# Moving eight background steps of a two-mixer encoder layer to later stages

## The chip, the core and the metric

The kernel runs on one core of a Trainium2 chip. Each engine of a core has a queue of its own and works it off in order: TensorE (PE) multiplies and transposes, VectorE (DVE), ScalarE (ACT) and GpSimd (POOL) do elementwise work, SyncE (SP) issues the DMA transfers. Where an instruction needs what another engine makes, it waits for a semaphore, and everything behind it on its own queue waits too. The metric is the time of one execution in microseconds (us), the median of several runs.

## The reference, cut to what matters

One layer is computed for a prompt of 1024 rows and a sample of 32 rows, width 1024, all in float32:

```
u  = RMSNorm(h) @ w_in                      # 1024 x 4096: q k v g for A and for B
oA = softmax(band(qA kA^T / 8 + bias)) vA   # 8 heads of 64, own chunk of 64 and 8 chunks back
oB = stick_breaking(qB kB^T / 8) vB         # 8 heads of 64, strictly causal:
     # w = sigmoid(z) * product of sigmoid(-z) over the later keys
y  = [oA * silu(gA), oB * silu(gB)] @ w_out
h  = h + RMSNorm(y)
h  = h + sigmoid(h @ w_ple_gate) * (p @ w_ple)
```

The new keys and values are outputs too. The sample rows attend to a cache of 512 keys.

## The kernel before

Float32 products are made of float32r products: each operand is split into a high and a low part, and three of the four products of parts are added (`mms`, L732; `multiply`, L1566).

The work has three parts. First the rows are normalised and turned, and the first three projections made. Then come eight *stages*, one for each head set in `pairs` (L1197): A0, B0, A1, B1, A2, B2, A3, B3. A head set is two heads of one mixer; two neighbouring stages (an A and a B) are a pair of head sets. Stage n holds the attention of head set n for both heads, and beside it the projections (`mm_...`) of head set n+1; stage 7 has the eight gate blocks (`mm_gA`, `mm_gB`) beside it. In the stages with an odd second number (2, 3, 6, 7) the attention of the sample rows is put in as well (`with_sample`, L1336). The third part makes the two large products with `w_out` and `w_ple_gate`.

For each row block of 128 queries the attention makes scores (`SA`, `SB`, L825), weights (`om`, `be`), the turned weights (`weights_t`, L871) and the product with the values (`PVA`, `PVB`). Most weight blocks are turned by PE: transposes into a bank `ptwA` or `ptwB`, then ACT casts the high part (`wTh`) and DVE subtracts the low part (`wTl`). There are two such banks. Row block 5 of A and blocks 4 and 6 of B (`ROUND`, L31) are turned through DRAM instead: DVE turns 32 x 32 squares, SP stores the result (`swapA<-om`) and loads it back with four transfers (`be<-swapA`), then ACT casts it.

The third part computes each product from quarters of the weights with seven instead of eight products of blocks (`ORDER`, L1499). For this it needs four sums and differences of the weight's quarters, T1 to T4. They are made beforehand, beside the attention, by eight steps: `sum_weights(w, kt)` (L1303) for `w` = "o" (`w_out`) and "g" (`w_ple_gate`) and `kt` = 0 to 3. A step loads four quarter slices of 128 x 512 (tiles `oB...` or `gB...`, buffers of the tag `sg`, of which there are three), does four subtractions or additions on POOL, each in two pieces of 128 x 256, and stores the four results to `sum_dr` in DRAM. The pieces have a lower standing than other POOL work (`rec.low = 1`). The buffers of the tag `sg` are later those of the gates' products (L754) and of the slices that the third part loads.

Two lists are merged for each stage (`weave`, L1265): `att`, the attention's steps, and `den`, the projections' steps, in proportion to the work that each entry states. The steps of weight sums are entries of `att` with stated work 0, at places 8 and 28 (`with_sums`, L1328).

Nothing is issued at once. All operations are recorded (`Recorder`, L265) and put in order by a planner (`order`, L381): it goes through all engines in planned time with stated costs, takes on each engine the ready operation of the best standing, and counts DVE and POOL work that shares a port one after the other. SP's transfers are planned as one line. The engines then execute in the planned order. So a step that is moved changes the order of nearly everything behind it. All instructions go through one line of the emitting function, L461, so the profile names groups by tile and not by line.

Of the kernel before, what the change touches and what calls it, by code (L numbers as in the profile page):

```python
# [466 lines left out]
def stream_step(  # L467
# [797 lines left out]
    def weave(att, den):  # L1265

        ta = sum(x[0] for x in att) or 1.0
        td = sum(x[0] for x in den) or 1.0
        ia = idn = 0
        pa = pd = 0.0  # L1270
        while ia < len(att) or idn < len(den):
            take_a = ia < len(att) and (idn >= len(den) or RATE * pa / ta <= pd / td)
            if take_a and att[ia][2] and any(x in prep for x in att[ia][2]):
                assert idn < len(den)
                take_a = False
            if not take_a and len(den[idn]) > 2 and den[idn][2]:
                take_a = ia < len(att)
            if take_a:
                rec.cls = 0
                att[ia][1]()  # L1280
                pa += att[ia][0]
                ia += 1
            else:
                rec.cls = 1
                den[idn][1]()
                pd += den[idn][0]
                idn += 1
            rec.cls = 0
            prepare()


    SUMS = {"T1": 0, "T2": 1, "T3": 2, "T4": 3}
    QUARTERS = {"B11": (0, HALF[0]), "B12": (0, HALF[1]), "B21": (4, HALF[0]), "B22": (4, HALF[1])}

    def weight_part(w, key, kt):
        if key in SUMS:
            return sum_dr[w][kt, SUMS[key]]
        k0, cols = QUARTERS[key]
        if w == "g":
            return w_gate[0].rearrange("(p k) c -> k p c", k=KD)[k0 + kt][:, cols]  # L1300
        return w_out[0, (k0 + kt) * P:(k0 + kt + 1) * P, cols]

    def sum_weights(w, kt):  # L1303
        b = {}

        def sub(out, x, y, op):
            rec.low = 1
            for c in (slice(0, 256), slice(256, 512)):
                nc.gpsimd.tensor_tensor(out[:, c], x[:, c], y[:, c], op)
            rec.low = 0  # L1310

        for key in ("B12", "B22", "B11", "B21"):
            b[key] = at2.tile([P, 512], F32, tag="sg", name=f"{w}{key}{kt}", bufs=3)
            rec.hold(b[key])
            dma(b[key], weight_part(w, key, kt))
            if key == "B22":
                sub(b[key], b[key], b["B12"], ALU.subtract)
                dma(sum_dr[w][kt, 2], b[key])
            if key == "B11":
                sub(b["B12"], b["B12"], b[key], ALU.subtract)  # L1320
                dma(sum_dr[w][kt, 0], b["B12"])
                sub(b[key], b["B22"], b[key], ALU.add)
                dma(sum_dr[w][kt, 1], b[key])
            if key == "B21":
                sub(b[key], b["B11"], b[key], ALU.subtract)
                dma(sum_dr[w][kt, 3], b[key])

    def with_sums(att, todo):  # L1328
        out = list(att)
        for i, (w, kt) in enumerate(todo):  # L1330
            out.insert(8 + i * 20, (0.0, lambda w=w, kt=kt: sum_weights(w, kt), None))
        return out
# [3 lines left out]
    def with_sample(att, steps):  # L1336
        out = list(att)
        for at_, st in reversed(list(zip(SAMPLE_AT, steps))):
            out.insert(at_, (st[0], st[1], None))
        return out  # L1340
# [67 lines left out]
    for n in range(8):  # L1408
        den = []
        for j in range(*span[n + 1]):  # L1410
            den += col_steps(j)
        att = seq[n, 0] + seq[n, 1]
        if pairs[n][1] % 2 == 1:
            att = with_sample(att, sample_attention(pairs[n][0], pairs[n][1] // 2))
        if n < 4:
            att = with_sums(att, [("og"[n // 2], 2 * (n % 2) + i) for i in range(2)])
        weave(att, den)


# [446 lines left out]
```

## Time and profile before

| | |
|---|---|
| median of 3 runs | 788.48 us (788.15 to 789.07) |
| the profiled execution | 791.73 us |
| its span | 789.9 us |
| PE / DVE / ACT / POOL busy | 777.9 / 590.3 / 532.2 / 472.3 us |
| granted clock of TensorE | 0.999 |
| data moved by DMA | 153.66 MB, mean 195 GB/s |

The profiled execution has its own time, a little above the median, and its span runs from the first instruction to the last. The page gives busy times by engine, the span in 40 slices with the busy share of each engine in tenths, the DMA queues, the chain of work that ended last, and the costliest groups of instructions. In a group, the figures behind the first bar are the busy time and the mean of one instruction in ns, and those behind the second are the engine's idle time just before them and what ended it. Idle time on an engine counts only if PE, busy for nearly the whole span, comes to wait for it.

### The profile page before, as it was taken

To read this page: it belongs to the slowest core of one execution; us is meant where nothing else is said; L and a number is where in the kernel's file an instruction comes from. 1 tells how busy PE (TensorE), PEld (TensorE's weight loads), DVE (VectorE), ACT (ScalarE), POOL (GpSimd) and SP (SyncE) were. 2 spreads that over 40 slices of the span, in tenths; PEclk is the share of its full clock that TensorE was granted. 3 is DMA by queue.
4 is the path that set the end of the run, shared out by engine and by line. 5 is a ranking of instruction groups with operands and counts; after the bars stand their busy time and mean duration, and the time that the engine had idled before them with its cause. 6 is when DMAs were issued, how large, how long until landed. Compare 5 with 4: busy or idle time off the path is not lost.

```text
span 789.9 us, 14445 instructions
## 1 busy us (share of the span) xinstructions
PE 777.9 (98%) x4606; PEld 718.7 (91%) x4606; DVE 590.3 (75%) x1105; ACT 532.2 (67%) x1169; POOL 472.3 (60%) x554
## 2 busy tenths in 40 slices
PE   9999999999999999999999999999999999999997
PEld 7999989999999999999999999999998787888786
DVE  7717677897788887777979778884464677988965
ACT  6636786786687766887677787753336966777651
POOL 5615776865677677644645465565562529599523
PEclk9999999999999999999999999999999999999999
DMA  8419876757786858743525756655588865859754
GB/s 303 133 41 276 207 219 188 223 150 221 201 238 207 226 174 250 162 122 119 146 65 173 175 133 183 186 165 164 144 275 287 277 190 186 298 164 345 273 161 134
DMA packets 161086, 153.66 MB, mean 195 GB/s; under 512 B 38561, under 2 KB 127177, under 8 KB 161010
## 3 DMA queue, kind: packets, MB, share of 16 engines
q1 hardware_dynamic: 161010, 152.73, 65.3%
q8 instruction: 37, 0.61, 0.3%
q14 instruction: 39, 0.32, 0.1%
HBM read 94.45 MB, written 49.83 MB: 183 GB/s over the span
## 4 chain that ended last, share of the span: by engine, by line
PE 86%; DVE 3%; ACT 3%; DMA 3%; POOL 2%; issue 1%; SPq 1%; ACTq 0%; DVEq 0%
PE mm_gB L461 6%; PE mm_gA L461 6%; PE mm_kB L461 5%; PE mm_qA L461 5%; PE mm_kA L461 5%; PE mm_vA L461 5%; PE mm_qB L461 5%; PE PVB L461 4%; PE mm_vB L461 4%; PE SA L461 4%; PE SB L461 4%; PE PVA L461 3%; PE ptwB L461 3%; PE g1P L461 2%; PE o3P L461 2%; PE o1P L461 2%
## 5 line engine op out<-in xcount | busy, mean ns | idle before, releaser
L461 POOL TENSOR_TENSOR be<-be,om 128x256 f32<-128x256 f32 (+8 forms) x66 | 81.6, 1240 | 66.2 <-DVE om L461 51.9
L461 DVE TENSOR_TENSOR_SCAN om<-om,SB 128x384 f32<-128x384 f32 (+5 forms) x96 | 92.2, 965 | 16.2 <-ACT be L461 7.6
L461 POOL TENSOR_SCALAR be<-be,statA 128x640 f32<-128x640 f32 (+3 forms) x64 | 45.0, 708 | 28.6 <-DVE statA L461 21.0
L461 ACT ACTIVATE om<-SB 128x384 f32<-128x384 f32 (+5 forms) x96 | 47.3, 499 | 20.7 <-DVE SB L461 15.7
L461 ACT ACTIVATE be<-SB 128x384 f32<-128x384 f32 (+5 forms) x96 | 46.7, 498 | 11.7 <-DVE om L461 6.8
L461 ACT ACTIVATE be<-om,statA 128x640 f32<-128x640 f32 (+3 forms) x64 | 44.6, 697 | 11.9 <-DVE statA L461 8.8
L461 DVE TENSOR_TENSOR wTl<-ptwA,wTh 128x512 fp32r<-128x512 f32 (+2 forms) x80 | 36.7, 481 | 8.3 <-ACT wTh L461 7.7
L461 ACT CAST wTh<-ptwA 128x512 fp32r<-128x512 f32 (+2 forms) x80 | 32.0, 425 | 10.4 <-PE ptwA L461 8.1
L461 DVE TENSOR_TENSOR wTl<-ptwB,wTh 128x512 fp32r<-128x512 f32 (+3 forms) x64 | 33.9, 545 | 5.8 <-ACT wTh L461 4.6
L461 DVE CUSTOM_DVE_ANT_0 om<-SA,biasA 128x320 f32<-128x320 f32 (+2 forms) x64 | 30.1, 482 | 9.0 <-PE SA L461 7.4
L461 DVE TENSOR_TENSOR wTl<-be,wTh 128x640 fp32r<-128x640 f32 (+1 forms) x24 | 31.6, 1318 | 6.3 <-ACT wTh L461 6.2
L461 ACT CAST wTh<-ptwB 128x512 fp32r<-128x512 f32 (+3 forms) x64 | 29.7, 483 | 8.2 <-PE ptwB L461 6.9
L461 PE MATMUL ptwA<-ident,be 128*128 128x128 f32 x200 | 32.7, 273 | 1.7 <-POOL om L461 1.4
L461 PE MATMUL SB<-kdB,LB 128*128 128x384 f32 (+5 forms) x96 | 33.0, 348 | 0.0
L461 PE MATMUL SB<-klB,LB 128*128 128x384 f32 (+5 forms) x96 | 32.6, 344 | 0.0
L461 PE MATMUL SA<-kdA,LA 128*128 128x320 f32 (+2 forms) x96 | 30.0, 322 | 0.9 <-DVE LA L461 0.8
L461 PE MATMUL ptwB<-ident,be 128*128 128x128 f32 x192 | 29.4, 273 | 0.2 <-DVE wTl L461 0.2
L461 PE MATMUL SA<-klA,LA 128*128 128x320 f32 (+2 forms) x96 | 29.3, 315 | 0.0
L461 POOL TENSOR_TENSOR oB<-oB,oB 128x256 f32<-128x256 f32 x32 | 25.7, 816 | 4.9 <-DVE om L461 3.8
L461 PEld LDWEIGHTS ptwA<-ident,be 128*128 128x128 f32 x200 | 24.5, 140 | 3.6 <-POOL om L461 1.7
L461 POOL TENSOR_TENSOR gB<-gB,gB 128x256 f32<-128x256 f32 x32 | 25.8, 824 | 1.8 <-DMA gB<-in_w_ple_gate_dram 1.8
L461 ACT CAST wTh<-be 128x640 fp32r<-128x640 f32 (+1 forms) x24 | 19.2, 799 | 8.2 <-DMA be<-swapA 5.3
(711 smaller groups left out, 2683.7 us busy)
## 6 DMA issues: line engine op xcount, KB each, us to landing
oB<-in_w_out_dram SPq DMA_DIRECT2D x16, 256.0 KB, 5.0
sum_dro<-oB SPq DMA_DIRECT2D x16, 256.0 KB, 2.2
gB<-in_w_ple_gate_dram SPq DMA_DIRECT2D x16, 256.0 KB, 4.0
sum_drg<-gB SPq DMA_DIRECT2D x16, 256.0 KB, 3.5
x<-in_x_prompt_dram SPq DMA_DIRECT2D x16, 256.0 KB, 4.5
h_dr<-h SPq DMA_DIRECT2D x8, 512.0 KB, 4.1
ht<-h_dr SPq DMA_DIRECT2D x8, 512.0 KB, 5.7
raw<-sum_drg SPq DMA_DIRECT2D x16, 256.0 KB, 3.6
```

The lines of the kernel that those rows point to most:

```text
L461: getattr(getattr(tc.nc, o.what[0]), o.what[1])(*args, **kw)
```

## The change

The two steps that stood beside each of the first four stages (0 to 3) are put beside others: a table names the stages and steps. Stage 2 holds the first two steps of `w_out`, stage 4 its last two, stage 5 the first two of `w_ple_gate` and stage 6 its last two. In pairs of head sets: none beside the first, two steps beside the second, four beside the third, two beside the fourth. The steps themselves, their places 8 and 28 in the list and their order are the same.

```diff
+    SUMS_AT = {2: [('o', 0), ('o', 1)], 4: [('o', 2), ('o', 3)], 5: [('g', 0), ('g', 1)], 6: [('g', 2), ('g', 3)]}
     SUMS = {"T1": 0, "T2": 1, "T3": 2, "T4": 3}
...
         att = seq[n, 0] + seq[n, 1]
         if pairs[n][1] % 2 == 1:
             att = with_sample(att, sample_attention(pairs[n][0], pairs[n][1] // 2))
-        if n < 4:
-            att = with_sums(att, [("og"[n // 2], 2 * (n % 2) + i) for i in range(2)])
+        att = with_sums(att, SUMS_AT.get(n, ()))
         weave(att, den)
```

## The prediction

> **What bounds the kernel now.** The page first: the span and each engine's busy time.
>
> ```profile
> span 789.9 us, 14445 instructions
> PE 777.9 (98%) x4606; PEld 718.7 (91%) x4606; DVE 590.3 (75%) x1105; ACT 532.2 (67%) x1169; POOL 472.3 (60%) x554
> PEclk9999999999999999999999999999999999999999
> DMA  8419876757786858743525756655588865859754
> ```
>
> TensorE is busy for 777.9 of 789.9 us at full granted clock. The change removes no matmul, so only the 12 us in which PE stands still can change, and new stillness can come. The second line of digits shows DMA fuller in the first half of the attention than in the second.
>
> Next, windows cut at the eight stages (stage n is the attention of the n-th head set, A when n is even, B when odd, beside the next set's projections; stage 7 stands beside the gates). Columns: length, busy time and count of PE, PEld, DVE, ACT, POOL, then clock, DMA share, GB/s.
>
> ```profile
> 63.00:125.00 62.00, 59.63 (x389) 57.47 (x388) 44.97 (x118) 45.01 (x105) 41.26 (x54) 1.00 0.80 223
> 125.00:177.00 52.00, 51.02 (x324) 49.24 (x323) 44.76 (x62) 38.97 (x84) 38.34 (x41) 1.00 0.70 199
> 177.00:247.00 70.00, 69.81 (x461) 66.98 (x462) 55.68 (x140) 51.83 (x125) 48.47 (x68) 1.00 0.77 216
> 247.00:301.00 54.00, 54.00 (x351) 52.33 (x351) 44.84 (x76) 39.51 (x91) 37.43 (x47) 1.00 0.69 200
> 301.00:363.00 62.00, 62.00 (x406) 60.28 (x405) 47.47 (x119) 47.88 (x111) 38.29 (x47) 1.00 0.63 163
> 363.00:415.00 52.00, 50.96 (x323) 49.33 (x322) 42.35 (x64) 36.68 (x82) 26.06 (x30) 1.00 0.44 122
> 415.00:478.00 63.00, 63.00 (x425) 61.42 (x424) 50.88 (x133) 49.52 (x118) 32.99 (x42) 1.00 0.61 160
> 478.00:601.00 123.00, 122.79 (x778) 120.12 (x776) 81.97 (x129) 63.79 (x144) 67.25 (x68) 1.00 0.62 191
> ```
>
> PE stands still for 2.4 us in stage 0, 1.0 in stage 1, 0.2 in stage 2, nothing in 3, 4 and 6, 1.0 in stage 5, 0.2 in stage 7. The wait view of PE, asked for stages 0, 1, 5 and 7, names them (one row is met in stage 1's end, one each in 5 and 7, the first three in stage 0):
>
> ```profile
> PE ptwA L461 <- POOL om L461: 1.4, 1, 1.4
> PE SA L461 <- DVE LA L461: 0.8, 1, 0.8
> PE ptwA L461 <- DVE wTl L461: 0.2, 1, 0.2
> PE mm_kB L461 <- ACT stvA L461: 1.0, 1, 1.0
> PE ptkA L461 <- DVE wTl L461: 1.0, 1, 1.0
> PE ptwB L461 <- DVE wTl L461: 0.2, 1, 0.2
> ```
>
> Where are the weight sums now? The tile view gives their pieces on POOL, the list of DMA issues their transfers, and the tile view of the sums in DRAM their first use:
>
> ```profile
> L461 POOL TENSOR_TENSOR oB<-oB,oB x32: 722/738/1632, 82.2 to 198.7; 128x256 f32<-128x256 f32 x32
> L461 POOL TENSOR_TENSOR gB<-gB,gB x32: 723/740/1725, 207.1 to 320.9; 128x256 f32<-128x256 f32 x32
> oB<-in_w_out_dram SPq DMA_DIRECT2D x16, 256.0 KB, 5.0
> sum_dro<-oB SPq DMA_DIRECT2D x16, 256.0 KB, 2.2
> L461 SPq DMA_DIRECT2D woT<-sum_dro x8: 327/430/842, 574.0 to 601.0; - x8
> ```
>
> They lie in stages 0 to 3, spill into 4, and are first read again at 574.
>
> One thing differs between A stages with sums and A stages without: how long ACT stands before it may cast a weight block that was turned through DRAM ("swap"). Groups of ACT asked for stages 0, 2, 4 and 6, in this order (the figure behind the second bar is the idle time before them, then who ended it):
>
> ```profile
> L461 ACT CAST wTh<-be 128x640 fp32r<-128x640 f32 x2 | 1.5, 728 | 5.0 <-DMA be<-swapA 2.8 <-POOL oB L461 2.2
> L461 ACT CAST wTh<-be 128x640 fp32r<-128x640 f32 (+1 forms) x3 | 2.4, 799 | 2.7 <-DMA be<-swapA 2.5 <-issue 0.2
> L461 ACT CAST wTh<-be 128x640 fp32r<-128x640 f32 (+1 forms) x4 | 3.1, 780 | 0.1
> L461 ACT CAST wTh<-be 128x640 fp32r<-128x640 f32 (+1 forms) x3 | 2.4, 793 | 0.0
> ```
>
> Landing of the swap's transfers (min/median/max) in the same four windows:
>
> ```profile
> DMA to landing us min/median/max: 2.4/4.2/5.5
> DMA to landing us min/median/max: 2.9/4.1/6.2
> DMA to landing us min/median/max: 2.2/3.0/4.0
> DMA to landing us min/median/max: 2.0/3.0/4.2
> ```
>
> With sums a swap transfer takes 4.1 to 4.2 us, without 3.0. The timeline of stage 0 shows how that reaches PE: ACT's queue stands behind the late block, and the casts that free PE's transpose banks come behind it.
>
> ```profile
> 115.26 0.73 ACT L461 CAST wTh<-be 128x640 fp32r<-128x640 f32 x1 [2.22 <-POOL oB L461]
> 115.89 0.74 ACT L461 CAST wTh<-ptwA 128x512 fp32r<-128x512 f32 x2
> 117.91 0.74 PE L461 MATMUL ptwA<-ident,be 128*128 128x128 f32 x5 [1.40 <-POOL om L461]
> ```
>
> The names behind the arrows are the last semaphores met. I read the cause as the late block: ACT has nothing else to wait for in those 2.22 us that its queue would not also have met in stages 4 and 6, where it stands for 0.1 and 0.0.
>
> **The change part by part.** A step is 4 loads, 4 stores and 8 POOL pieces. A pair of steps is 16 transfers of 256 KB (4.2 MB) and 16 pieces at 0.74 us, 11.8 us of POOL. Before, pairs stand in stages 0, 1, 2, 3; after, in 2, 4, 5, 6. Stage 2 keeps a pair (of w_out instead of w_gate, same size): 0. PE, ACT and DVE get no instruction more or less, but the recording layer reorders all of them from stage 0 on; I cost that at 0 in itself.
>
> Stage 0 loses its pair. Its waits of 1.4 and 0.2 us at 113 to 118 go: -1.6. The 0.8 at LA stays, since it ends at 65 and the first piece starts at 82.2. What would be late next there is nothing above 0.2.
>
> Stages 1 and 3 lose theirs: 0 (bounds -1.0 and 0). Stage 3 has no PE wait to lose. Stage 1's 1.0 us stands behind ACT's own queue, and stage 5 has a wait of the same size with no sums.
>
> Stage 5, a B stage, gains a pair. Its cover is room on POOL: 26.1 + 11.8 = 37.9 us of 52, as in stage 1 (38.3), and DMA: 122 + 81 GB/s (4.2 MB in 52 us), share 0.44 x 203/122 = 0.73, as in stage 1 (0.70). B stages with sums hold 1.0 and 0 of PE waits, the one without 1.0: 0, bounds 0 to +1.0.
>
> Stages 4 and 6, A stages, gain a pair each. POOL has room in both: at most 38.3 + 11.8 = 50 of 62 and 33.0 + 11.8 = 45 of 63. The cover that goes is the quick swap. DMA in stage 4: 163 less 17 (four spilled transfers of 256 KB go) plus 68 is 214 GB/s, share 0.63 x 214/163 = 0.83; in stage 6: 160 + 67, share 0.61 x 227/160 = 0.87. In the changed order one to two sum transfers stand in SP's queue between a swap's store and the last of its four loads, in both stages, and a store among them makes SP wait for POOL first:
>
> ```profile
> SPq L461 <- POOL oB L461: 13.7, 9, 3.0
> ```
>
> Two rows bound one such stage: stage 2, where the 2.7 us of ACT idle reached PE with nothing that the waits name, and stage 0, where 1.6 of 5.0 did. Their shares were 0.77 and 0.80; 0.83 and 0.87 are nearer to 0.80, so I take stage 0's price twice: +3.2 (bounds 0 and, if all of ACT's 5.0 reached PE, +10).
>
> Stage 7: the last step's fourth load and two pieces now stand among the first gate's instructions, and its rooms are those that the gates' products take next. I let the 0.2 us wait at stage 7's start come a second time: +0.2 (bounds 0 and +1.5, two pieces in front of the block that PE turns next). The sums land some 80 us before the read at 574: 0.
>
> Sum: -1.6 + 0 + 0 + 3.2 + 0.2 = +1.8 us. The profiled execution took 791.73 us, its span 789.9 and 1.8 around it, 3.3 over the median of 788.48; the difference is carried to the median: 790.3.
>
> **A rule against it.** DVE is the other neighbour of POOL. A two-input operation beside a POOL subtraction took 3.51 us, and the like of it in stage 0 takes 1.22:
>
> ```profile
> 61.48 3.51 DVE L461 TENSOR_TENSOR LA<-stqA,LA 64x1024 fp32r<-64x1024 f32 x1 [3.74 <-ACT LA L461]
> 105.19 1.22 DVE L461 TENSOR_TENSOR LB<-stqB,LB 64x1024 fp32r<-64x1024 f32 x1
> ```
>
> If this is how sums cost, B stages pay, where DVE is fullest: 44.8 us busy with sums (stages 1 and 3), 42.4 without (5), and 47.5 in A stage 4. One loaded B stage fewer would then be worth up to 2.4 us: 786.1. [...]
>
> **The rivals.**
> Room in the late stages (ends faster). DMA is so much emptier in stages 4 and 6 that two more transfers among many leave the swap within ACT's slack, as in stage 2. Then only the -1.6 is left: 786.9, and 785.9 if stage 1's 1.0 goes too. For it: stage 2 hid its 2.7. Against: worked shares above stage 0's. It decides where ACT's idle before a swapped block stays under about 2.7 us a stage.
> One of the two pays: +0.2, 788.7.
> Sums cost by the port: 786.1, above.
> SP's queue (ends slower still). The first gates' weights are loaded at the end of stage 6:
>
> ```profile
> L461 SPq DMA_DIRECT2D wr_gA<-in_w_in_dram x8: 384/468/1276, 463.2 to 513.2; - x8
> 469.45 1.14 ACT L461 CAST wh_gA<-wr_gA 128x512 fp32r<-128x512 f32 x2
> L461 PE MATMUL mm_gA<-hnh,wh_gA x96: 317/323/406, 478.8 to 542.5; 128*128 128x352 f32 x96
> ```
>
> They are ready at 470.6 and used at 478.8: 8.2 us of slack. After the change two stores that wait for POOL and four loads of sums come shortly before. Four waits of 3.0 us would use 12, 3.8 more than the slack: 788.48 + 1.8 + 3.8 = 794.1.
>
> **How the numbers follow.** Forecast 0.45 (own range 789.3 to 792.0, some 0.1 of it under 790.06), one pays 0.20, room 0.15, port 0.07, SP's queue 0.13. About 0.2% (1.6 us) is what a measurement of this kernel can tell from no change. Faster: nearly all of room and port, 0.20. Slower: 0.35 + 0.13 = 0.48. Same: the rest, 0.32. The range runs from just below the room case to short of the SP case, leaving out less than 0.1 on each side: 786.0 to 793.8.
>
> **What would show it.** Right: ACT's idle before be<-swapA gone from stage 0 and back, 2.5 us or more, in stages 4 and 6; PE idle near 0.8 in stage 0 and 1 to 2 us in stages 4 and 6; swap landing near 3 us in stage 0 and over 4 in stages 4 and 6; DMA shares 0.8 and above there. Wrong: stages 4 and 6 with PE idle 0 in spite of slower swaps (ACT had slack), or new waits in stage 5 or at the gates' start.

## The result, and the profile after

The changed kernel took 794.36 us (median of 4 executions, 794.24 to 796.76) against 788.78 us of the kernel before beside it: a ratio of 1.0078, 95% interval 1.0064 to 1.0092 (the ratios here and below differ a little from the quotients of the two medians). It is slower, which had the largest of the three chances (0.48), and by 5.6 us, three times the forecast's 1.8. A second set of 6 executions, taken with the last experiments, has a median of 793.07 (790.62 to 795.23) and a ratio of 1.0055 (1.0037 to 1.0073). Its width of 4.6 us is part of the answer below.

The profiled execution took 794.24 us. Its page begins:

```profile
span 792.5 us, 14437 instructions
...
PE 778.3 (98%) x4606; PEld 719.3 (91%) x4606; DVE 588.0 (74%) x1105; ACT 531.0 (67%) x1169; POOL 474.8 (60%) x554
```

TensorE's work is the same (778.3 us busy, 777.9 before). The windows of the changed kernel, cut at its own stages 0 to 7, have the columns named in the prediction:

```profile
63.00:122.00 59.00, 58.21 (x384) 56.67 (x383) 43.70 (x114) 43.80 (x103) 28.80 (x39) 1.00 0.62 170
122.00:174.00 52.00, 51.81 (x328) 49.92 (x327) 42.55 (x66) 39.68 (x86) 30.91 (x30) 1.00 0.50 135
174.00:238.00 64.00, 64.00 (x428) 62.25 (x429) 48.63 (x133) 47.32 (x115) 45.30 (x62) 1.00 0.72 206
238.00:297.00 59.00, 59.00 (x386) 57.31 (x385) 48.58 (x81) 42.00 (x100) 29.30 (x36) 1.00 0.51 142
297.00:356.00 59.00, 58.64 (x383) 56.96 (x383) 47.34 (x115) 46.79 (x104) 43.94 (x55) 1.00 0.78 216
356.00:415.00 59.00, 55.90 (x344) 53.87 (x343) 44.60 (x68) 38.84 (x90) 39.42 (x48) 0.97 0.58 170
415.00:480.00 65.00, 63.44 (x421) 61.17 (x420) 51.33 (x131) 48.03 (x112) 44.61 (x55) 1.00 0.76 214
480.00:604.00 124.00, 123.86 (x785) 121.16 (x784) 83.77 (x132) 65.98 (x151) 70.12 (x74) 1.00 0.65 199
```

The sums have arrived where the change puts them: POOL falls to 29 to 31 us in stages 0, 1 and 3 and rises to 44, 39 and 45 in stages 4, 5 and 6. PE stands 0.8 us in stage 0, 0.4 in stage 4, 3.1 in stage 5 and 1.6 in stage 6. Stage 5 is also the only one whose granted clock is not 1.00. PE's waits by name:

```profile
PE PVB L461 <- ACT wTh L461: 3.1, 1, 3.1
PE SB L461 <- DVE LB L461: 1.9, 2, 1.6
...
PE SA L461 <- DVE LA L461: 0.8, 1, 0.8
PE mm_kB L461 <- ACT stvA L461: 0.2, 1, 0.2
```

**Stage 5.** The timeline of the changed kernel shows one chain over four engines (start, length, engine, operation, idle before it and who ended that):

```profile
380.65 1.49 SPq L461 DMA_DIRECT2D be<-swapB  x3
383.30 3.12 POOL L461 TENSOR_TENSOR wl_vA<-wr_vA,wh_vA 128x512 fp32r<-128x512 f32 x2
...
386.52 0.73 POOL L461 TENSOR_TENSOR gB<-gB,gB 128x256 f32<-128x256 f32 x1
387.28 0.35 SPq L461 DMA_DIRECT2D gB<-in_w_ple_gate_dram  x1
387.67 0.43 SPq L461 DMA_DIRECT2D be<-swapB  x1
391.36 0.94 ACT L461 CAST wTh<-be 128x896 fp32r<-128x896 f32 x1 [4.39 <-DMA be<-swapB]
392.36 1.21 PE L461 MATMUL PVB<-wTh,v2B 128*128 128x512 f32 x4 [3.10 <-ACT wTh L461]
```

SP issues three of the four loads of a swapped block. The next operation on its queue is a load of the weight sums, into the tile `gB210`, and that needs a buffer of the tag `sg`. The buffer comes free with a sum piece on POOL, which waits for its turn behind two `wl_vA`. SP's wait view, asked for 372 to 395 us, gives the stand:

```profile
SPq L461 <- POOL gB L461: 6.4, 2, 5.0
```

So the fourth load of the swap goes out 5 us late, lands late, ACT stands 4.4 us, PE 3.1. Behind it, the windows of the changed kernel show something that no window of the kernel before has while PE still works:

```profile
392.00:396.00 4.00, 3.65 (x15) 3.41 (x16) 2.00 (x2) 2.59 (x8) 4.00 (x6) 0.67 0.72 195
396.00:400.00 4.00, 4.00 (x23) 3.74 (x23) 2.92 (x3) 3.18 (x8) 1.94 (x2) 0.90 0.70 221
```

PE is busy, but at a granted clock of 0.67 and 0.90: (0.33 + 0.10) x 4 us = 1.7 us of work not done.

**Stage 6.** The timeline again:

```profile
461.32 1.44 POOL L461 TENSOR_TENSOR gB<-gB,gB 128x256 f32<-128x256 f32 x2
462.83 2.39 POOL L461 TENSOR_TENSOR klB<-stkB,kdB 64x1024 fp32r<-64x1024 f32 x1
462.90 3.41 DVE L461 TENSOR_TENSOR LB<-stqB,LB 64x1024 fp32r<-64x1024 f32 x1
466.36 0.33 PE L461 MATMUL SB<-kdB,LB 128*128 128x128 f32 x1 [1.56 <-DVE LB L461]
```

POOL's `klB` stands behind two sum pieces and begins 0.07 us ahead of DVE's `LB`, which then takes 3.41 us instead of the 1.22 shown in the prediction, and here that reaches PE: `SB` stands 1.56 us for it. In the two profiles of the kernel before, `klB` had ended when `LB` began, at 463.60 against 464.17 and at 460.60 against 461.17, and `LB` took 1.22 us in both.

**The swaps of A.** Landing of the swap's transfers in stages 0, 2, 4 and 6 of the changed kernel, and ACT's group in stages 4 and 6:

```profile
DMA to landing us min/median/max: 2.2/2.6/3.1
DMA to landing us min/median/max: 2.6/3.6/4.6
DMA to landing us min/median/max: 2.5/4.4/4.7
DMA to landing us min/median/max: 2.2/3.7/4.6
```

```profile
L461 ACT CAST wTh<-be 128x640 fp32r<-128x640 f32 (+1 forms) x4 | 3.1, 785 | 0.1
L461 ACT CAST wTh<-be 128x640 fp32r<-128x640 f32 (+1 forms) x3 | 2.4, 792 | 0.0
```

The transfers became slower there (3.0 before), but ACT waits 0.1 and 0.0 us: the block comes in time all the same.

### The profile page after: what moved, and what is told of

Read it like the earlier page. It is cut to its first block, busy times and chain, and to the rows that moved or that the text cites. A ratio compares the mean times of both kernels' runs of the same rounds, so it can differ in the third digit from the quotient of the medians.

```text
span 792.5 us, 14437 instructions
## 1 busy us (share of the span) xinstructions
PE 778.3 (98%) x4606; PEld 719.3 (91%) x4606; DVE 588.0 (74%) x1105; ACT 531.0 (67%) x1169; POOL 474.8 (60%) x554
## 4 chain that ended last, share of the span: by engine, by line
PE 88%; DVE 4%; POOL 2%; ACT 2%; DMA 2%; issue 1%; SPq 0%; DVEq 0%; ACTq 0%; POOLq 0%
PE mm_gA L461 6%; PE mm_kB L461 6%; PE mm_qB L461 6%; PE mm_gB L461 5%; PE mm_kA L461 5%; PE mm_vB L461 5%; PE mm_qA L461 4%; PE PVB L461 4%; PE SB L461 4%; PE mm_vA L461 4%; PE SA L461 4%; PE PVA L461 3%; PE ptwA L461 3%; PE g1P L461 2%; PE o3P L461 2%; PE o1P L461 2%
## 5 line engine op out<-in xcount | busy, mean ns | idle before, releaser
L461 POOL TENSOR_TENSOR be<-be,om 128x256 f32<-128x256 f32 (+8 forms) x66 | 85.4, 1299 | 80.6 <-DVE om L461 39.4
L461 POOL TENSOR_SCALAR be<-be,statA 128x640 f32<-128x640 f32 (+3 forms) x64 | 46.6, 735 | 43.3 <-DVE statA L461 38.1
L461 DVE CUSTOM_DVE_ANT_0 om<-SA,biasA 128x320 f32<-128x320 f32 (+3 forms) x64 | 30.1, 483 | 8.6 <-PE SA L461 7.2
L461 DVE TENSOR_TENSOR wTl<-be,wTh 128x640 fp32r<-128x640 f32 (+1 forms) x24 | 29.4, 1227 | 6.4 <-ACT wTh L461 6.4
L461 DVE STREAM_TRANSPOSE om<-be 128x640 f32<-128x640 f32 (+1 forms) x24 | 22.2, 925 | 4.9 <-POOL be L461 4.2
```

Source lines behind the costliest of these rows:

```text
L461: getattr(getattr(tc.nc, o.what[0]), o.what[1])(*args, **kw)
```

## The experiments

The ratios are to the kernel before on the same chip, with 95% intervals. *First theory*: SP's stand in front of one swap makes stage 5 late, and the lower clock follows from PE's stop. *Rival*: the later stages are too full, so a pair of steps costs there whatever the order.

### The kernel before again: x_before

No edit.

> The kernel before, once more, under another name. Its first profiled execution took 791.73 us, 3 us above its median of 788.78, while the changed kernel's took 794.24 against a median of 794.36. If the 3 us were that one execution's own, this profile shows a time within 0.7 us of 788.8 and, beside the changed kernel's profile, the full loss of 5.6 us; where the first profile was slower tells which stage the 3 us belong to. If the profile itself costs the kernel before 3 us, it shows 791.7 again. The timed ratio is 1.000 either way.

Measured: 788.93 us (787.57 to 790.51), ratio 0.9997 (0.9986 to 1.0008), profile 788.65. Its window of stage 0:

```profile
63.00:122.00 59.00, 58.22 (x383) 56.56 (x381) 44.19 (x116) 45.00 (x104) 39.60 (x54) 1.00 0.82 233
```

PE stands 0.8 us there, as in the changed kernel (58.21 of 59). The wait of 1.4 us at `ptwA`, on which the forecast's gain rested, is not in this execution at all. From its first product to the next stage's, stage 0 took 61.6 us in the first profile, 59.6 in this one and 58.8 in the changed kernel. So 2 of the 3 us by which the first profile lay above the median were spent in stage 0 of that one execution.

### One pair of issues swapped: x_onemove

```diff
  SP: be<-swapB x3
- SP: gB210 <- w_ple_gate
- SP: be<-swapB
+ SP: be<-swapB
+ SP: gB210 <- w_ple_gate
```

> The changed kernel with one pair of issues in SyncE's queue swapped: the gate's piece gB210, which waits for a room of POOL, is issued behind the fourth part of be<-swapB in stage 5 and not ahead of it. Nothing else moves. Theory (the queue's head stands and the swap behind it comes late): TensorE's 3.1 us before PVB and the 1.7 us of lower granted clock behind it go, so 794.4 - 4.8 = 789.6, between 789 and 791.3 (the wait gone and the clock's loss left). Rival (the stage is late because one more pair of steps fills POOL and the transfers there; the wait only shows it): the wait turns up somewhere else in stage 5, 793 to 794.4.

Measured: 788.32 us (787.43 to 792.15, 12 executions), ratio 0.9990 (0.9974 to 1.0005). At the median the whole loss is gone with one pair of issues, though the order of every other engine and the place of all sums are those of the changed kernel. The timeline:

```profile
381.03 2.19 SPq L461 DMA_DIRECT2D be<-swapB  x4
387.26 0.97 ACT L461 CAST wTh<-be 128x896 fp32r<-128x896 f32 x1
387.70 0.35 SPq L461 DMA_DIRECT2D gB<-in_w_ple_gate_dram  x1
```

SP still stands until 387.7, but with nothing behind it that PE needs soon. The rival falls: nothing else in stage 5 takes the wait's place. The first theory foretold 789 to 791.3, a little too high.

The profiled execution of this kernel was one of its longest, 791.89 us. Its stage 6 has the collision of `klB` and `LB` (`LB` 3.40 us, a stop of 1.54 us), and this window right behind it:

```profile
464.00:468.00 4.00, 4.00 (x19) 4.00 (x18) 3.51 (x8) 3.02 (x7) 4.00 (x5) 0.57 0.46 131
```

That is 0.43 x 4 = 1.7 us again. Of 12 executions nine lie between 787.4 and 789.2 and three at 790.4, 791.9 and 792.2, and these three have the lowest mean clock (0.998, 0.997, 0.997 against 0.999 or 1.0).

### One sum piece earlier on POOL: x_pool

```diff
+ POOL: gB110 <- sum, second piece
  POOL: wl_vA x2
  POOL: memsets
- POOL: gB110 <- sum, second piece
```

> The changed kernel with SyncE's order as it is; on GpSimd one sum piece (the second into gB110) goes ahead of the two subtractions wl_vA of stage 5, which took 3.12 us and whose result TensorE reads 15 us later. Theory (SyncE's issue of gB210 waits for that piece to free the room, and the piece waits for nothing but its turn): the issue goes out 3.1 us earlier, the fourth part of the swap lands 3.1 us earlier, TensorE's 3.1 us before PVB go and the dip of the clock with them: as with the swapped issues, 787.5 to 789.5. Rival (the room is freed by something else, or the piece's own load is late): SyncE's wait stays near 5 us and the time at 794 to 796.

Measured: 787.95 us (787.60 to 788.60, 11 executions), ratio 0.9994 (0.9985 to 1.0003). The timeline:

```profile
383.32 1.31 POOL L461 TENSOR_TENSOR gB<-gB,gB 128x256 f32<-128x256 f32 x1
384.66 0.35 SPq L461 DMA_DIRECT2D gB<-in_w_ple_gate_dram  x1
388.60 0.95 ACT L461 CAST wTh<-be 128x896 fp32r<-128x896 f32 x1 [2.85 <-DMA be<-swapB]
389.60 1.19 PE L461 MATMUL PVB<-wTh,v2B 128*128 128x512 f32 x4
```

SP's order is untouched, with the gate's load still ahead of the swap's last part. The load goes out 0.03 us after the piece ends, 2.6 us earlier than in the changed kernel, and PE does not stop. So the buffer that SP waited for is the one this piece frees. ACT still stands 2.85 us for the swap without cost: that much slack was there, and 4.4 was too much. Stage 6 of this profile shows how near the other collision is:

```profile
457.98 1.22 DVE L461 TENSOR_TENSOR LB<-stqB,LB 64x1024 fp32r<-64x1024 f32 x1
458.36 3.10 POOL L461 TENSOR_TENSOR klB<-stkB,kdB 64x1024 fp32r<-64x1024 f32 x1 [0.95 <-POOL gB L461]
```

Here `LB` comes first and takes its 1.22 us; `klB` takes the longer time (3.10 us, 2.40 in the kernel before), and nothing waits for it. Of the eight profiles with this order in stage 6 (the changed kernel twice, x_onemove, x_pool and the four with repeated casts below), `klB` began first in two, the first of the changed kernel and that of x_onemove, and only these have the stop. This is the best version of the study. It is 6.4 us below the changed kernel's first median, and not to be told from the kernel before.

### Less overlap in stage 6: x_both

The swapped issues, and on POOL:

```diff
+ POOL: klB
  POOL: gB223 <- sum, two pieces
- POOL: klB
```

Here the store of that sum goes out ahead of the two pieces, so one of the 32 stored sums is unfinished and the output isn't the reference's.

> The swapped issues of stage 5, and in stage 6 GpSimd's klB ahead of the two sum pieces into gB223, so that it begins about 0.6 us earlier, when its operand kdB is ready, and overlaps DVE's LB the less. If LB took 3.4 us in place of 1.2 because klB ran beside it, LB ends 0.6 to 0.7 us earlier, TensorE's stop of 1.54 us in stage 6 falls to 0.8 or 0.9, and the dip of the clock to 0.57 seen behind it in one execution becomes rarer: 787.0 to 788.0, with no execution near 792. If LB's duration has nothing to do with klB: 788.3, and executions at 790 to 792 as before.

Measured: 788.51 us (787.72 to 791.95), ratio 1.0005 (0.9994 to 1.0017). Inconclusive. In its profile `LB` came first (458.03, 1.22 us), so the collision did not occur, but executions at 791.0 and 791.95 did, with mean clocks of 0.998 and 0.996. What slowed these was not seen.

### One pair moved from stage 1 to stage 5: x_at0235

```diff
- SUMS at stages 0, 1, 2, 3
+ SUMS at stages 0, 2, 3, 5
```

> The kernel before with one pair of steps alone moved: that of stage 1 goes to stage 5 (the pairs stand beside stages 0, 2, 3 and 5). In its order on SyncE no piece of the gate stands between the four parts of be<-swapB of stage 5's second half. If a pair beside stage 5 costs 4 to 5 us as such (density): 792.8 to 793.6. If the loss hangs on that one place in the order alone: 788.8, between 788 and 789.5, and stage 5 shows no wait of TensorE over 1 us.

Measured: 800.0 us (798.21 to 802.76), ratio 1.0138 (1.0117 to 1.0160). Neither forecast holds. Stage 5, with its pair, is 52.4 us long from its first product to the next stage's, 55.5 in the second profile of the kernel before and 59.4 in the changed kernel. Stage 4 is 63.7 us long against 58.6, but some 20 products have moved into it out of stage 5 (407 and 325 against 384 and 346), so the two have to be taken together: 116.1 us against 114.1, and 1.7 of the 2.0 are a dip of the clock at the start of stage 4. So a pair beside stage 5 costs next to nothing by its presence. The largest loss is in stage 3 (65.1 against 59.4 us), which keeps a pair: PE waits 0.4 to 0.9 us four times, for the sample rows' values and for score and weight blocks, then 2.3 us at its end for `wh_kB`, with the dip to 0.58 behind it.

### Stage 5's pair back to stage 3: x_at2346

```diff
- SUMS at stages 2, 4, 5, 6
+ SUMS at stages 2, 3, 4, 6
```

> The changed kernel with stage 5's pair of steps beside stage 3 in its place (pairs beside stages 2, 3, 4 and 6). By the trace of the changed kernel the 4.8 us of stage 5 go and the 1.6 us of stage 6 (k sum of DVE beside POOL) may stay or go: 794.4 - 4.8 = 789.6, or 788.0 without stage 6's; with stage 0 rid of its pair it could beat the kernel before, which the traces' 3.0 us for stage 0 would put at 787. The forecast's own price of 1.6 us for stage 4 and for stage 6 gives 789 to 790. The rival that any pair in a later stage costs some 2 us more than in an early one gives 791 to 793.

Measured: 791.41 us (790.74 to 792.73), ratio 1.0028 (1.0017 to 1.0040). That is inside the 791 to 793 of the rival by which any pair in a later stage costs some 2 us, and 1.8 above the first theory. The rival's price doesn't stand all the same: x_pool, with its four pairs in stages as late or later, ran at 787.95. Stage 5 falls to 54.1 us, as expected. Several waits of 0.3 to 0.7 us in stage 6 and one of 0.7 in stage 7 are new; stage 6 is 65.3 us long against 63.7 in the second profile of the kernel before.

### One pair from stage 3 to stage 6, one from stage 0 to stage 4: x_at0126 and x_at1234

```diff
- SUMS at stages 0, 1, 2, 3
+ SUMS at stages 0, 1, 2, 6        # x_at0126
+ SUMS at stages 1, 2, 3, 4        # x_at1234
```

> The kernel before with stage 3's pair of steps alone moved to stage 6 (pairs beside stages 0, 1, 2 and 6); up to stage 3 the order is that of the kernel before. The forecast's step: stage 6 takes 1.6 us longer by a late swap, 790.4, no stage else changed. The reading so far (a pair beside stage 6 has room of its own; only where GpSimd's klB begins ahead of DVE's LB do 1.5 to 1.8 us come in): 788.8 where klB comes second, 790.5 where it comes first, with ScalarE waiting less than 1 us for a swap in stage 6. If an order drawn anew is a lottery, as in the two cases of 800 and 803: anything from 788 to 803, with waits of several kinds from stage 3 on.

> The kernel before with stage 0's pair of steps moved to stage 4 (pairs beside stages 1 to 4). The forecast's steps: stage 0 loses 1.6 us and stage 4 gains 1.6, 788.8. By the traces so far stage 0 loses 0.8 to 0.9 (the second profile of the kernel before had no wait of 1.4 us there) and stage 4 gains 0 to 0.5: 788.0 to 788.6. If an order drawn anew is a lottery: up to 803, and the loss stands in stages that neither lost nor gained a pair.

Measured: 788.61 us for the first, ratio 1.0000 (0.9991 to 1.0009), and 802.47 for the second, ratio 1.0154 (1.0131 to 1.0177). The first refutes the price of 1.6 us for a pair beside stage 6. The second loses over 5 us in each of stages 1 and 3, neither of which gained or lost a pair, and stage 0 is 0.8 us shorter (58.8 against 59.6). Its two longest waits:

```profile
PE PVB L461 <- DVE wTl L461: 2.4, 1, 2.4
PE mm_kB L461 <- ACT wh_kB L461: 1.6, 1, 1.6
```

The profile of x_at0126 has a wait of 1.2 us before `ptwA` at 117 us, in the part whose order is that of the kernel before: stage 0's wait comes and goes. It goes with the swap. These are ACT's casts of the swapped blocks in stage 0, in x_before and in x_at0126:

```profile
L461 ACT CAST wTh<-be 128x640 fp32r<-128x640 f32 x2 | 1.5, 732 | 1.7 <-DMA be<-swapA 1.7
L461 ACT CAST wTh<-be 128x640 fp32r<-128x640 f32 x2 | 1.5, 727 | 4.7 <-DMA be<-swapA 4.7
```

Where ACT stands 5.0 and 4.7 us (the first profile of the kernel before, and this one), PE waits 1.4 and 1.2; where it stands 1.7 and 2.4 (x_before and x_at0235), PE doesn't wait there. In the changed kernel ACT stands 0.0.

### The sums' work of lower standing: x_low

```diff
+            rec.low = 1
             dma(b[key], weight_part(w, key, kt))
+            rec.low = 0
```

The pieces on POOL have had this lower standing all along, so only the loads change theirs.

> The changed kernel with the sum steps' loads and GpSimd pieces of lower standing in the order (they go only where nothing else of their engine is ready). In SyncE's order no load of the gate's pieces stands between the four parts of be<-swapB in stage 5's second half. If the loss of the change is that place in the queue: 787 to 790, and stage 5 near 55 us. If late pairs cost by their mere load on GpSimd and the transfers: 792 to 794. A new wait of another kind can come in, because the whole order is drawn anew.

Measured: 803.2 us (801.96 to 805.74), ratio 1.0187 (1.0169 to 1.0206), the slowest of all. Stage 5 takes 54.1 us, as expected, with the same pairs at the same stages. But stage 3, which holds no pair, takes 64.2 us, and stage 7 takes 130.5 instead of 122, with stops of 1.8 and 3.4 us among the products of `mm_gA` and a half clock for 6.8 us behind the first.

### The sums left out: x_none

```diff
- SUMS at stages 2, 4, 5, 6; third part reads T1 to T4
+ no sums; third part reads plain quarters
```

> The weight sums are left out altogether (no loads, no GpSimd pieces, no stores), and the last stage loads plain quarters of the weights in their place, so what it computes isn't the reference's. It gives the price of hiding all eight steps. From the kernel before, by TensorE's waits of its two profiles in stages 0 to 3 (0.8, 1.0): 786.5 to 788.5, that is 0.5 to 2.5 us under before. If the sums cost nothing where they stood before: 789. If the placement of the rest, ordered anew, matters more than the sums: anything from 787 to 795.

Measured: 789.55 us (789.03 to 790.41), ratio 1.0011 (1.0002 to 1.0020). Not faster. That 64 transfers and 64 POOL pieces cost nothing where the kernel before has them is the likely reading, but it is not shown: this order is drawn anew as well, and has a stop of 1.5 us before `mm_kB` at 413 us where the kernel before has none. What is shown is that leaving all the steps out brought no gain.

### A stop made on purpose: x_stop3, x_stop5, x_stop5b, x_stop7

On x_pool, one ScalarE cast of stage 2 is repeated:

```diff
  ACT: wTh <- be, 128x896        # at 183 us
+ ACT: wTh <- be, 128x896        # x 3, 5 or 7, the same values
```

> A measurement of a stop by itself, on the version whose one GpSimd piece was moved (787.95 us, no dip of the clock in its profile, 11 executions within 1.0 us). ScalarE does one cast at 183 us, which TensorE's PVB reads at 185.9, three times more (the same values again; 0.9 us each, 1.7 us of slack). TensorE should stop 1.0 us there. If a stop costs its length alone: 789.0. If any stop of 1 us also brings a dip of the clock: 790.7.

> The same with five casts more: TensorE should stop 2.8 to 3.0 us at 186 us, far from the place where the change made it stop, with no transfer late and no wait in SyncE's queue behind it. If the dip of the granted clock to 0.5 that followed the 3.1 us stop of the changed kernel comes from the stop: a dip within 2 us behind it, and 787.95 + 2.9 + 1.7 = 792.5, between 792 and 793. If the dip came from something else at that place: no dip, and 790.8.

> The kernel with five casts more, for a second profile: in the first TensorE stopped 3.4 us and no dip of the clock followed (790.93 us), while the five executions without a profile took 792.0 to 793.7. If a stop of this length brings the dip in some executions only, a profile of 792 or more shows it within 2 us behind the stop, at 0.5 for about 3.4 us, and one below 791.5 shows none. If those executions were slower for another reason, a profile of 792 or more shows no dip.

> Seven casts more: TensorE should stop 5.6 to 6.0 us at 186 us. If a dip is certain once the stop is long enough: 787.95 + 5.8 + 1.7 = 795.4, in every execution (spread under 1.5 us), with the dip in the profile. If the dip stays a matter of chance: 793.7 in some executions and 795.4 in others.

Measured: 789.63 us for three casts more (stop 1.0 us, no dip in its profile; 0.7 over what the length alone would give), 792.74 for five and 792.68 in its second set, 796.23 for seven (795.58 to 796.70 in all four). Windows of the first and second profile of the kernel with five casts more, whose stop was 3.40 us in both, cut into stretches of 3.41 us for a reason given in the last section:

```profile
183.79:187.20 3.41, 1.73 (x12) 1.43 (x10) 1.32 (x3) 3.28 (x5) 0.38 (x1) 1.00 0.92 237
187.20:190.61 3.41, 1.69 (x9) 1.52 (x10) 1.09 (x1) 2.22 (x3) 0.00 (x0) 1.00 0.52 198
```

```profile
186.52:189.93 3.41, 0.07 (x1) 0.07 (x1) 0.09 (x1) 3.19 (x4) 0.00 (x0) 1.00 0.84 276
189.93:193.34 3.41, 3.41 (x10) 3.04 (x11) 1.17 (x2) 1.75 (x3) 1.26 (x2) 0.50 0.38 122
```

The same kernel, the same stop: once no dip, at 790.93 us, once a dip of 0.50 x 3.41 = 1.7 us, at 793.05. With seven casts more, PE stops 5.0 us, and the dip is twice as long:

```profile
190.43:197.26 6.83, 6.08 (x17) 5.24 (x18) 1.25 (x2) 2.46 (x4) 3.86 (x6) 0.50 0.50 163
```

PE is busy for 6.08 us of it, so 3.0 us of work are lost: 787.95 + 5.0 + 3.0 = 796.0, near the measured 796.23, where the expectation had counted a single dip (795.4). All four executions have a mean clock of 0.995 or 0.996. So the dip follows from the stop, in some executions at 3.4 us and, as far as four executions tell, always at 5.0.

### The changed kernel again: x_after

No edit.

> The changed kernel once more, for more executions beside the kernel before and for a second profile. If its loss is the late swap of stage 5 with the clock's dip behind it, and the collision of klB and LB in stage 6: again a stop of about 3.1 us before PVB, and 793.5 to 796.8. If the dip of 1.7 us comes only in some executions, these spread over 2 us or more (the fastest near 792.7) and the lowest have a granted clock of 0.998 or above.

Measured: 793.07 us (790.62 to 795.23). The profile is that of the fastest execution. It has the stop before `PVB` and neither the dip nor the collision, as a window and two rows of the timeline show:

```profile
392.00:396.00 4.00, 3.82 (x22) 3.48 (x23) 2.69 (x4) 3.62 (x11) 4.00 (x6) 1.00 0.84 230
```

```profile
460.71 1.22 DVE L461 TENSOR_TENSOR LB<-stqB,LB 64x1024 fp32r<-64x1024 f32 x1
461.09 3.10 POOL L461 TENSOR_TENSOR klB<-stkB,kdB 64x1024 fp32r<-64x1024 f32 x1 [0.76 <-POOL gB L461]
```

Stage 5 is 1.6 us shorter than in the first profile and stage 6 2.1 us; the executions differ by 794.24 - 790.62 = 3.6.

Together: the change's loss is a stop of 3.0 to 3.1 us, in both profiles (787.95 without it, 790.62 with it alone), and two parts that come in some executions only, the dip of 1.7 us behind the stop and the collision in stage 6, 1.6 to 2 us. The first is shown by two edits, the dip by the repeated casts. That of the collision is read from the profiles that have it and those that haven't; the edit meant to show it (x_both) was inconclusive. Of the changed kernel's ten executions the two below 791 us have a mean clock of 0.999, the other eight, at 792.9 and above, 0.996 or less.

## Why the prediction was wrong, step by step

- **Stage 0, -1.6 us: the chain held, the size did not.** PE's wait does come with a late swap, and ACT's idle there is gone in the changed kernel (0.0). But of the four profiles with a pair beside stage 0 only two have the wait (1.4 and 1.2 us). Against the second profile of the kernel before, the changed kernel's stage 0 is 0.8 us shorter, and PE stands 0.8 us in both. The step that carried a difference found in one profiled execution over to the median failed here: that execution stood 3.3 us above the median, and the wait to be gained is not in every execution.
- **Stages 1 and 3, 0 (bounds -1.0 to 0): right.** Stage 1's wait at `mm_kB` fell from 1.0 to 0.2 us, inside the bounds. That it stood behind ACT's own queue, so that no sums could matter to it, was not the whole reason.
- **Stage 5, 0 (bounds 0 to +1.0): this step failed the most.** The cover it named was there: POOL at 39.4 us (forecast 37.9), DMA share 0.58 (forecast 0.73). What decided wasn't among the covers: the place of one load in SP's queue. The forecast looked for sum transfers between the parts of a swap in stages 4 and 6 alone. Measured in its place: a stop of 3.0 to 3.1, and 1.7 more where the dip follows it. The wait of 1.0 us at `ptkA` that the stage had before is gone, so on balance it grew from 55.5 us to 57.8 without the dip and 59.4 with it.
- **Stages 4 and 6, +1.6 each through late swaps: wrong in mechanism.** The swap's transfers landed later, as said (3.0 to 4.4 and 3.7), and DMA shares rose (0.63 to 0.78, 0.61 to 0.76; forecast 0.83 and 0.87). But ACT waited 0.1 and 0.0 us for them. This is what the prediction named as its refutation. The step that failed is the carrying over of stage 0's price: there a late swap reaches PE, here ACT had the slack. Stage 4 got 0.4 us by `LB`; stage 6 got 1.6 in one profile, where `LB` took 3.41 us beside `klB`, and none in another, where it took 1.22. A pair beside stage 6 alone (x_at0126) cost 0.
- **Stage 7, +0.2: nothing to be seen of it.** PE stands 0.1 us in stage 7, and 0.2 before; the bounds (0 to +1.5) hold.
- **Reordering at 0 in itself: wrong.** This is the largest error of principle. Placements with the same work ran at 788.6, 791.4, 800.0 and 802.5 us, and the same placement with another standing at 803.2. Leaving the steps out gained nothing (x_none).
- **The rule weighed:** that DVE's two-input work takes longer beside POOL's was expected, if at all, to make B stages faster without sums. It came as a loss in an A stage, where sum pieces pushed `klB` onto `LB`. No run shows the port that the chances name; what the runs show is `LB` at 3.41 and 3.40 us where `klB` began 0.07 us ahead of it (the changed kernel, x_onemove), and at 1.22 where `LB` began first (x_pool, x_after).
- **The rivals:** SP's queue, given 0.13, had the right kind of cause (SP stands for POOL, and what PE needs is behind it), at the wrong place, the gates' weights. That its 794.1 lies 0.3 us from the first median is luck: PE stands 0.1 us in stage 7. Room in the late stages was right for stages 4 and 6, and nothing was to be gained by it.

The forecast's 790.3 lies near the fastest executions of the changed kernel, 790.6 and 790.8, but that is luck too: wrong steps offset each other. The first median lies 0.6 us above the range, the second inside it.

Two things stay open. What in the redrawn orders makes stage 1 or 3, or both, lose 5 us each (and stage 7 of x_low 8) was seen in part as waits for late casts, and not traced to its origin; so these larger losses are not explained by anything here. And the two longest executions of x_both were not profiled.

## What to carry to other kernels

Where work is put in the background of a scheduled kernel, its volume may cost little and its place in one in-order queue several us (here 788.32 and 787.95 us, x_onemove and x_pool, against 794.36 with the same steps beside the same stages): for each moved transfer that needs a buffer, look up who frees the buffer, what stands ahead of that on its engine, and which urgent transfer is queued behind. The cure is then one moved instruction (here one sum piece ahead of two subtractions not needed for some 15 us), and need not be another placement. And a wait that a single profile shows is worth its cost only if a second profile shows it too.

## What the runs showed of the hardware that was not expected

In these runs a stop of TensorE could cost more than its length. Behind stops of 1.54, 2.26, 2.41, 3.10 and 3.40 us (x_onemove, x_at0235, x_at1234, the changed kernel, x_stop5b) the granted clock went to half for 3.41 us, 1.7 us of work each time, and behind those of 5.0 (x_stop7) and of 1.8 and 3.4 close together (x_low) for 6.83. Behind others it did not: 1.54 (x_none), 1.56 (the first profile of the changed kernel, in stage 6, and x_at0235), 1.65 (x_at1234, x_low), 3.02 (the second profile of the changed kernel) and 3.40 (x_stop5).

What looks like chance goes in part with the place of the stop. In the changed kernel the dip lasts 3.41 us and begins at 393.40 us, 395.94 us ahead of the fall of the clock that ends the execution (789.34): 116 steps of 3.413 us. In x_stop5b it is 600.74 us (189.93 and 790.67), 176 such steps, and the dip of x_stop7 lasts two (6.83). If an execution is laid out in such steps back from that fall, TensorE stood 2.38 us of the step right ahead of the dip in the changed kernel, and 3.34 in x_stop5b. The stop of x_stop5, as long as that of x_stop5b, fell across a border, 1.68 and 1.72, and no dip followed. In the stages of the kernel before TensorE never stood more than 1.40 us of a step, and no dip came. The exception is x_onemove: a dip behind 1.54, where x_none's 1.54 and x_at1234's 1.64 brought nothing. This is read from the profiles afterwards; no run moved a stop within the steps on purpose, and what sets the steps, or halves the clock, no run shows.
